# U units beside the context's score steps, and their Gelu in the expert stage

## The chip, the cores and the metric

The kernel runs on one core of one Trainium2 chip. The metric is the device time of one execution in microseconds (us), the median of some runs. The core has five engines, each with its own queue of instructions, worked off in order: TensorE (PE; its weight loads are shown apart as PEld), VectorE (DVE), ScalarE (ACT), GpSimd (POOL) and SyncE (SP), which issues most of the loads.

## The reference

Two blocks stand one after the other. The first has retention, a gated unit, and a layer of 16,384 experts of which every token uses 128. The second has two mixer layers, each with window attention, latent attention and a gated convolution, over 512 tokens and a context of 256. Its context doesn't depend on the first block.

```python
def block(hb):                       # the expert layer, over 128 tokens
    ...                              # expert, g: 8 heads x 16 experts, softmax
    ue = expert_u[expert]
    act = jax.nn.gelu(jnp.einsum('td,thkd->thk', hb, ue), approximate=False) * g
    ve = expert_v[expert]
    return jnp.einsum('thk,thkd->td', act, ve)

if update_ctx:                       # the first mixer layer's own work on the context
    ya_c = ctx_gqa_attn(qa_c.reshape(B, L, H_A, HD_A), kac, vac, sink)
    yb_c = ctx_mla_attn(qn_c, qr_c, kn_c, krb_c, vb_c)
    yc_c = short_gated_conv(bc_c, cc_c, uc_c, conv_w)
    out_c = merge_branches(ya_c, yb_c, yc_c, za_c, zb_c, zc_c, ga_c, gb_c, gc_c, w_branch, w_o)
```

## The kernel before

Every fp32 operand is split into a high and a low part, and every product is three matmuls (`mm3`, `fm`, L95). ScalarE casts the high part, and GpSimd or VectorE subtracts it to get the low one (`split`, L120 and L122).

The experts are computed densely for 384 of the tokens (TD) and sparsely, by gathered rows, for the other 128. The dense part has three stages. First `up_products` makes 128 *units* (U): for each block of 128 experts it loads 512 KB of weights in two parts (`wr<-eu`), splits them (`wh`, `wl`), makes 24 matmuls of 384 columns into `u`, and ScalarE evacuates them with a Gelu into `hb` (L745); two units' `hb` go to DRAM (`hd`). It is a generator, and each `next` issues one unit. Then `route` picks the experts and writes the gates to DRAM (`gd`). Last, `experts` runs 32 groups of four blocks: it loads gates `gt`, `ht` (four units' values from `hd`) and four tiles `vr`, multiplies `at = ht * gt`, splits `at` and `vr`, and adds up into eight PSUM banks `acc`.

Units are issued in the shadow of other work: `tick(n)` adds n to a counter and issues a unit for each whole one. `route` has its own amounts (R1 to R3). `context`, the first mixer layer's work on the context, runs between `route` and the experts: projections, convolution, gates, latent attention, gates, window attention, gates, output. Each weight product there asks for a PSUM bank by `mm()`, which ticks R4 = 0.53 and issues 0.95 sparse steps (`self.sparse`: a gather `sg` by GpSimd, and a multiply by VectorE, into `dots` or `sacc`). What units are left run after the context (`unit`, and the loop behind `cs.close()`). The two attentions are functions that the second block's layers call too; both take a `tick` of the caller's, and `context` gives none, so there the default does nothing.

A *score step* is one block of 128 queries of one head: score matmuls into `cs`, then on VectorE maximum `mx` and bias `nb`, on ScalarE the exponential `p` (L1124), on TensorE its transposition `ct` (L1138), which ScalarE and VectorE split into `pt`, and after two steps the weighting of the values `cv`. The context has 16 steps in each attention. ScalarE holds one set of functions at a time; an `ACT_TABLE_LOAD` stands where the next function is in another one than the last, as with Gelu and Exp.

A scheduling layer sets the final order on each engine: instructions that stand later in the code may go ahead of those that wait. Context weights are loaded into two buffers (`wrc`), split into `whc` and `wlc`, the latter by VectorE.

Of the kernel before, what the change touches and what calls it, by code (L numbers as in the profile page):

```python
# [14 lines left out]
AF = mybir.ActivationFunctionType  # L15
# [1 line left out]
AX = mybir.AxisListType  # L17
PSUM = bass.MemoryType.PSUM

R1, R2, R3, R4, R5, R6 = 0.5, 0.7, 0.6, 0.53, 0.9, 0.12  # L20
PC = 2
MB, MD, MR = 4, 2, 1.15
TG, NT = 4, 8
T = 512
TC = 256
# [3 lines left out]
TD = 384  # L29
# [38 lines left out]
class Kern:  # L68
# [507 lines left out]
    def experts(self):  # L576
        nc, a, h = self.nc, self.a, self.h
        self.fine = ("",)
        with ExitStack() as s1:
# [4 lines left out]
            ws = (up, 2 * PC, 3, "")  # L584
# [39 lines left out]
            ps = ExitStack()  # L624
            acc = [self.pool("pacc%d" % c, 1, PSUM, ps).tile([128, T], F32, name="acc%d" % c) for c in range(8)]

            for g in range(32):
                gt, ht = first if g == 0 else inputs(g)
                if g == 8:
                    self.load(x, self.x1d)  # L630
                ops = []
                for q in range(4):
                    raw = vp.tile([128, D], F32, name="vr", tag="vr", bufs=3)
                    self.load(raw, a["ev"][g * 4 + q])
                    vl = vp.tile([128, D], F32R, name="vl", tag="vl", bufs=4)
                    vh = vp.tile([128, D], F32R, name="vh", tag="vh", bufs=4)
                    self.split(vh, vl, raw, pool=False)
                    al = vp.tile([128, TD], F32R, name="al", tag="al", bufs=4)
                    at = vp.tile([128, TD], F32, name="at", tag="at", bufs=2)
                    nc.vector.tensor_tensor(at.rearrange("p (b t) -> p b t", t=32), ht[:, q, :].rearrange("p (b t) -> p b t", t=32),  # L640
                                            gt[:, :, q, :], op=OP.mult)
                    ah = vp.tile([128, TD], F32R, name="ah", tag="ah", bufs=4)
                    self.split(ah, al, at, pool=False)
                    ops.append((vh, vl, ah, al))
                    if g < 31:
                        for c in range(8):
                            cs = slice(c * 128, (c + 1) * 128)
                            self.mm3(acc[c][:, :TD], vh[:, cs], vl[:, cs], ah, al, g == 0 and q == 0, False)
                    self.sparse(S5)
# [82 lines left out]
    def up_products(self, ws, up, pu):  # L732

        for g in range(16):
            for q in range(4):
                hb = up.tile([128, 2, TD], F32, name="hb", tag="hb", bufs=2)
                for i in range(2):
                    w = self.wget(ws, self.a["eu"][g * 8 + q * 2 + i].rearrange("p (k n) -> p k n", k=8), 8, 128)
                    ps = pu.tile([128, T], F32, name="u", tag="u")
                    if self.last_units:  # L740
                        with self.tc.issue_after(self.pe_last()):
                            self.fm(ps[:, :TD], w, 0, 128, self.h, 0, TD)
                    else:
                        self.fm(ps[:, :TD], w, 0, 128, self.h, 0, TD)
                    self.nc.scalar.activation(out=hb[:, i, :], in_=ps[:, :TD], func=AF.Gelu)  # L745
                    if i == 1:
                        self.store(self.hd[g][:, 2 * q:2 * q + 2, :], hb)
                    yield
# [425 lines left out]
    def latent_attention(self, ws, l, sp, mm, sc, tp, pv, h, tq, kv, nk, kr, yy, bufs, pm, tick=lambda n: None):  # L1174

        nc = self.nc
# [7 lines left out]
        for j in range(2):  # L1184
            w = self.win(ws, l, "vb%d" % j)
            for n in range(0, nb, 2):
                ps = pm()
# [57 lines left out]
            nc.gpsimd.tensor_tensor(rot[0], rot[0], t, op=OP.add)  # L1245

        lag = 1 if tq == T else 0
        late = Later()

        def head(pr, e, n0, q, sz, rs):  # L1250
# [12 lines left out]

            for n in (n0, n0 + 1):
                qs = slice(n * 128, (n + 1) * 128)
                tick(R6)
                ps = sc()
                for lo, hi in spans:
                    self.mm3(ps[:, lo:hi], q[0][:, qs], q[1][:, qs], kt[0][:, lo:hi], kt[1][:, lo:hi], True, True)
                p = self.numer(sp, ps, 0, nk, SB, None, rs[:, n, e:e + 1])  # L1270
                late.now += 1
                late.after(lag, lambda n=n, p=p: turn(n, p))
                if n > n0:
                    late.after(2 * lag, values)
                late.run()
# [4 lines left out]
        for pr in range(4):  # L1280
            if pr == 1 and tq == T:
                self.dve_lo = ()
            if pr == 0:
                rope(0, pm)
                kn = keys(0, pm)
                ps = nope(0, pm)
# [62 lines left out]
    def window_attention(self, ws, l, sp, mm, sc, tp, pv, h, tq, kz, va, yy, bufs, tick=lambda n: None):  # L1349
        nc = self.nc  # L1350
# [18 lines left out]
            return self.silu2(ws, l, "za%d" % j, sp, "sza", bufs, mm, h, tq)  # L1369

        nq_, nsz = query(0), gate(0)
        tick(3)
        self.halves = False
        for j in range(4):
            q, sz = nq_, nsz
# [2 lines left out]
            for e in range(2):  # L1378
                sink = self.nsink[:, 8 * l + j + 4 * e:8 * l + j + 4 * e + 1]
                for n0 in range(0, nq, 2):  # L1380
# [3 lines left out]
                    for n in (n0, n0 + 1):  # L1384
# [11 lines left out]
                                mm_(ps[:, c:c + 128], self.identb, self.bmask[:, mi, :], start=False, stop=i == len(edge) - 1)  # L1396
                        for i in range(2):
                            mm_(ps[:, off:off + TC], q[e][:, qs], kz[e][i][:, off:off + TC], start=i == 0, stop=i == 1)
                        tick(R5)
                        slots = blocks + [vo, vo + 1]  # L1400
                        used.append(slots)
                        p = self.numer(sp, ps, lo, off + TC, SA, sink, rs[:, n, e:e + 1], es[:, n, e:e + 1])
# [43 lines left out]
    def context(self, ws, pu, tick, unit):  # L1446
        nc, a = self.nc, self.a
        with ExitStack() as s1:
# [20 lines left out]
            for l in range(1):  # L1469
# [9 lines left out]
                with ExitStack() as s2:  # L1479
# [27 lines left out]
                    self.conv(ws, l, sp, mm, h, TC, y)  # L1507
                    self.gates(ws, l, 2, True, mt, y, sp, mm, h, TC)
                    y = sp.tile([128, 2, 4, TC], F32R, name="cy", tag="cy")
                    self.latent_attention(ws, l, sp, mm, sc, tp, pv, h, TC, kv, TC, kr, y, 1, mm)  # L1510
                    self.gates(ws, l, 1, False, mt, y, sp, mm, h, TC)
                    kz = [[sp.tile([128, TC], F32R, name="ckz%d%d" % (i, k), tag="kt%d%d" % (i, k)) for k in range(2)] for i in range(2)]
                    self.pack_keys(kz, 0, TC, ka)
# [1 line left out]
                    for n in range(2):  # L1515
                        self.split(va[:, n, :, 0, :], va[:, n, :, 1, :], vf[:, n, :].rearrange("p (e c) -> p e c", e=2))
                    y = sp.tile([128, 2, 4, TC], F32R, name="cy", tag="cy")
                    self.window_attention(ws, l, sp, mm, sc, tp, pv, h, TC, kz, va, y, 1)
                    self.gates(ws, l, 0, False, mt, y, sp, mm, h, TC)
                    ot = sp.tile([128, 8, TC], F32, name="cot", tag="cy")  # L1520
                    x = sp.tile([128, 8, TC], F32, name="cx", tag="v", bufs=1)
# [416 lines left out]
```

## Time and profile before

| | us |
|---|---|
| median of 3 runs | 3709.58 (3703.13 to 3713.91) |
| the profiled execution | 3703.34 |
| its span | 3701.6 |
| route, to about | 1090 |
| context, about | 1090 to 1702 |
| last units, to | 1744 |
| experts, to about | 2290 |

The profile is of one execution. Its span goes from the first instruction to the last. TensorE's mean granted clock over it was 0.966 of full speed. Engines' busy times overlap, so that they don't add up to the span.

### The profile page before, as it was taken

How to read it: one execution, taken by the hardware profiler on the slowest of the kernel's cores; microseconds unless marked ns; L12 is line 12 of the kernel's file. 1: busy time of each engine (PE TensorE's matmuls, PEld its weight loads, DVE VectorE, ACT ScalarE, POOL GpSimd, SP SyncE). 2: the span in 40 equal slices, each digit the busy share in tenths (PEclk: the TensorE clock that was granted, in tenths of full speed). 3: DMA queues.
4: the chain of work that ended last, by engine and by line, in shares of the span. 5: the costliest groups of instructions: out<-in, count | busy, mean ns of one | idle time of the engine just before them, and what ended most of it. 6: DMA issues, size and time to landing. Idle time of an engine off the chain costs nothing.

```text
span 3701.6 us, 54609 instructions
## 1 busy us (share of the span) xinstructions
PE 3415.2 (92%) x20219; PEld 3074.3 (83%) x20219; DVE 2369.2 (64%) x4572; ACT 1564.2 (42%) x2940; POOL 1407.8 (38%) x1178
## 2 busy tenths in 40 slices
PE   6999999978889998897999999899999979999998
PEld 5889788877788988897999998778878877787777
DVE  7876865698867765666777775444255664433554
ACT  3323223235654374642333333444346443442663
POOL 2210114352235667565222211554425335542442
PEclk9999999989999998998999999999999989999999
DMA  7667644337877856578999993322211321212122
GB/s 274 217 204 263 219 159 152 107 125 269 298 265 242 301 194 241 184 273 294 355 342 337 327 328 111 103 69 69 77 52 55 134 82 63 75 67 67 54 72 99
DMA packets 273243, 668.18 MB, mean 181 GB/s; under 512 B 25424, under 2 KB 88016, under 8 KB 270160
## 3 DMA queue, kind: packets, MB, share of 16 engines
q1 hardware_dynamic: 220256, 469.43, 36.9%
q0 software_dynamic: 36864, 134.23, 10.1%
q10 hardware_dynamic: 15856, 61.02, 4.3%
q8 instruction: 159, 2.61, 0.3%
q14 instruction: 108, 0.88, 0.1%
HBM read 601.47 MB, written 63.11 MB: 180 GB/s over the span
## 4 chain that ended last, share of the span: by engine, by line
PE 65%; DVE 13%; DMA 7%; issue 7%; ACT 5%; POOL 3%; SPq 0%; POOLq 0%; ACTq 0%; DVEq 0%
PE mm L95 16%; PE acc L95 12%; PE gm L95 10%; PE u L95 8%; PE cm L95 4%; PE uq L95 2%; PE sc L95 2%; PE pv L1168 2%; DMA wr<-eu 2%; PE tp L1138 2%; PE pv L95 2%; PE tp L95 1%; DVE wm L212 1%; DVE wl L122 1%; POOL wl L122 1%
## 5 line engine op out<-in xcount | busy, mean ns | idle before, releaser
L122 POOL TENSOR_TENSOR wl<-wr,wh 128x512 fp32r<-128x512 f32 (+3 forms) x358 | 499.0, 1411 | 452.3 <-ACT wh L120 437.6
L120 ACT CAST wh<-wr 128x512 fp32r<-128x512 f32 (+3 forms) x546 | 355.8, 665 | 576.2 <-PE mm L95 201.5
L95 PE MATMUL u<-hh,wh 128*128 128x384 f32 (+1 forms) x1040 | 361.5, 348 | 31.8 <-ACT hb L745 31.6
L95 PE MATMUL u<-hh,wl 128*128 128x384 f32 (+1 forms) x1040 | 360.2, 347 | 9.7 <-DVE wl L122 8.9
L95 PE MATMUL u<-hl,wh 128*128 128x384 f32 (+1 forms) x1040 | 358.8, 345 | 0.0
L95 PE MATMUL acc<-ah,vh 128*128 128x384 f32 x1024 | 343.9, 336 | 8.8 <-ACT hb L745 8.8
L95 PE MATMUL acc<-al,vh 128*128 128x384 f32 x1024 | 343.3, 335 | 0.9 <-DVE al L122 0.9
L95 PE MATMUL acc<-ah,vl 128*128 128x384 f32 x1024 | 343.2, 335 | 0.0
L714 POOL DMA_INDIRECT sg<-ev,xid x128 | 153.3, 1198 | 311.4 <-DVE sacc L729 258.0
L120 ACT CAST vh<-vr 128x1024 fp32r<-128x1024 f32 x128 | 134.6, 1052 | 316.8 <-issue 145.0
L714 POOL DMA_INDIRECT sg<-ur,xid x128 | 146.8, 1147 | 270.2 <-DVE sg L212 250.7
L95 PE MATMUL mm<-hh,wh 128*128 128x512 f32 (+2 forms) x608 | 239.3, 398 | 9.1 <-DVE sm L432 4.2
L122 DVE TENSOR_TENSOR wl<-wr,wh 128x1024 fp32r<-128x1024 f32 (+4 forms) x188 | 179.5, 972 | 101.2 <-ACT wh L120 100.1
L95 PE MATMUL mm<-hh,wl 128*128 128x512 f32 (+2 forms) x608 | 238.9, 393 | 5.6 <-DVE wl L122 4.5
L95 PE MATMUL mm<-hl,wh 128*128 128x512 f32 (+2 forms) x608 | 238.8, 393 | 5.4 <-POOL hl L122 5.4
L122 DVE TENSOR_TENSOR vl<-vr,vh 128x1024 fp32r<-128x1024 f32 x128 | 158.3, 1237 | 128.4 <-ACT vh L120 126.9
L95 PEld LDWEIGHTS u<-hh,wh 128*128 128x128 f32 x1040 | 203.6, 196 | 34.8 <-ACT hb L745 32.9
L95 PEld LDWEIGHTS u<-hh,wl 128*128 128x128 f32 x1040 | 203.3, 196 | 13.1 <-DVE wl L122 11.3
L729 DVE SCALAR_TENSOR_TENSOR sacc<-sg,wts,sacc 128x1024 f32<-128x1024 f32 x128 | 189.3, 1479 | 22.5 <-DMA sg<-ev,xid 19.0
L95 PEld LDWEIGHTS u<-hl,wh 128*128 128x128 f32 x1040 | 203.4, 196 | 0.4
L95 PEld LDWEIGHTS acc<-ah,vh 128*128 128x128 f32 x1024 | 193.1, 189 | 9.3 <-ACT hb L745 9.1
L95 PEld LDWEIGHTS acc<-al,vh 128*128 128x128 f32 x1024 | 193.1, 189 | 1.1 <-DVE al L122 1.1
(713 smaller groups left out, 9837.2 us busy)
## 6 DMA issues: line engine op xcount, KB each, us to landing
wr<-eu SPq DMA_DIRECT2D x256, 256.0 KB
vr<-ev SPq DMA_DIRECT2D x128, 512.0 KB
wm<-wmod SPq DMA_DIRECT2D x88, 512.0 KB
wr<-w SPq DMA_DIRECT2D x164, 256.0 KB
wr<-wA SPq DMA_DIRECT2D x80, 512.0 KB
wrc<-w SPq DMA_DIRECT2D x79, 512.0 KB
wrg<-w SPq DMA_DIRECT2D x104, 256.0 KB
hd<-hb ACTq DMA_DIRECT2D x64, 384.0 KB
```

Of the source, the lines that this page charges most:

```text
L95: ins = self.nc.tensor.matmul(ps, l, r, start=first and i == 0, stop=last and i == 2)
L120: nc.scalar.copy(hi, x)
L122: eng.tensor_tensor(lo, x, hi.bitcast(F32), op=OP.subtract)
L212: return self.nc.vector.scalar_tensor_tensor(chunk, chunk, 1.0, row, op0=OP.mult, op1=OP.mult, accum_out=dst)
L714: self.here(nc.gpsimd.indirect_dma_start(t, None, tabs[i], bass.IndirectOffsetOnAxis(idx[:, j:j + 1], 0)))
L729: self.here(nc.vector.scalar_tensor_tensor(acc, t, wts[:, j:j + 1], acc, op0=OP.mult, op1=OP.add))
L1138: nc.tensor.transpose(t[:, (b - i) * 128:(b - i + 1) * 128], p[:, b * 128:(b + 1) * 128], self.ident)
L1168: nc.tensor.matmul(o[:, lo:hi], v(b), pt[k][:, b, lo:hi], start=i == 0 and k == 0, stop=i == len(parts) - 1 and k == 1)
```

## The change

The counter's amounts change, and score steps get one of their own, R9 = 1.0: `context` now hands its `tick` to both attentions. In the latent attention it issues a unit after the scores of each step, in the window attention too, and one ahead of the window attention. Each product of the context ticks 0.25 in place of 0.53. The evacuation of a unit becomes a copy, and the expert stage applies the Gelu to four blocks at once, in place, on the loaded `ht`. The other callers of the attentions keep what they had.

```diff
-R1, R2, R3, R4, R5, R6 = 0.5, 0.7, 0.6, 0.53, 0.9, 0.12
+R1, R2, R3, R4, R5, R6, R9 = 0.5, 0.7, 0.6, 0.25, 0.9, 0.12, 1.0
...
                 gt, ht = first if g == 0 else inputs(g)
+                nc.scalar.activation(out=ht, in_=ht, func=AF.Gelu)
...
-                    self.nc.scalar.activation(out=hb[:, i, :], in_=ps[:, :TD], func=AF.Gelu)
+                    self.nc.scalar.copy(hb[:, i, :], ps[:, :TD])
...
         lag = 1 if tq == T else 0
+        more = tick if tq < T else lambda n: None
         late = Later()
...
             for n in (n0, n0 + 1):
                 qs = slice(n * 128, (n + 1) * 128)
-                tick(R6)
+                if tq == T:
+                    tick(R6)
                 ps = sc()
                 for lo, hi in spans:
                     self.mm3(ps[:, lo:hi], q[0][:, qs], q[1][:, qs], kt[0][:, lo:hi], kt[1][:, lo:hi], True, True)
+                more(R9)
...
-        tick(3)
+        tick(3 if loc else 1)
...
-                        tick(R5)
+                        tick(R5 if loc else R9)
...
-                    self.latent_attention(ws, l, sp, mm, sc, tp, pv, h, TC, kv, TC, kr, y, 1, mm)
+                    self.latent_attention(ws, l, sp, mm, sc, tp, pv, h, TC, kv, TC, kr, y, 1, mm, tick)
...
-                    self.window_attention(ws, l, sp, mm, sc, tp, pv, h, TC, kz, va, y, 1)
+                    self.window_attention(ws, l, sp, mm, sc, tp, pv, h, TC, kz, va, y, 1, tick)
```

What this does to the order is best seen at three places. On TensorE, in the window attention (`cs` scores, `u` a unit, `ct` transpositions of `p`), two heads' scores stood together before, with 21 of a unit's matmuls behind them:

```order
L1398 MATMUL cs<-ckz_14404,aql 128x256
L1398 MATMUL cs<-ckz_14405,aql 128x256
L1398 MATMUL cs<-ckz_14404,aql 128x256
L1398 MATMUL cs<-ckz_14405,aql 128x256
L95 MATMUL u<-hh,wh 128x384
...
L95 MATMUL u<-hh,wl 128x384
L1138 MATMUL ct<-c_ident,p 128x128 x2
L1398 MATMUL cs<-ckz_14402,aqh 128x256
L1398 MATMUL cs<-ckz_14403,aqh 128x256
```

After the change each step's scores are followed by the 24 matmuls of one unit and then by that step's transpositions:

```order
L1402 MATMUL cs<-ckz_14219,aql 128x256
L1402 MATMUL cs<-ckz_14220,aql 128x256
L95 MATMUL u<-hh,wh 128x384
...
L95 MATMUL u<-hh,wl 128x384
L1139 MATMUL ct<-c_ident,p 128x128 x2
L1402 MATMUL cs<-ckz_14219,aql 128x256
L1402 MATMUL cs<-ckz_14220,aql 128x256
```

The units moved to between the scores and the transpositions that wait for them. On SyncE, in the projections and the convolution ahead of the first score step, the loads of context weights (`wrc`) and of units (`wr<-eu`) stood so before:

```order
L87 DMA wrc<-w 128x1024 x3
L87 DMA wr<-eu 128x512 x2
L87 DMA wrc<-w 128x1024 x8
L87 DMA wr<-eu 128x512 x2
L87 DMA wrc<-w 128x1024 x3
L87 DMA wr<-eu 128x512 x2
L87 DMA wrc<-w 128x1024 x2
L87 DMA wr<-eu 128x512 x2
```

And so after it:

```order
L87 DMA wrc<-w 128x1024 x3
L87 DMA wr<-eu 128x512 x2
L87 DMA wrc<-w 128x1024 x13
L87 DMA wr<-eu 128x512
L87 DMA wrc<-w 128x1024 x3
L87 DMA wr<-eu 128x512
L87 DMA wrc<-w 128x1024 x10
L87 DMA wr<-eu 128x512 x2
```

Unit loads went from one pair to two or three products to one pair to some thirteen. On ScalarE, where the units end and the experts begin (`ah`, `vh` are the experts' casts), the last three evacuations stood among the experts' casts before:

```order
L120 CAST wh<-wr 128x512
L120 CAST ah<-at 128x384 x2
L120 CAST vh<-vr 128x1024
L745 ACTIVATE hb<-u 128x384
L90 DMA hd_96<-hb 128x768
L120 CAST vh<-vr 128x1024 x2
L745 ACTIVATE hb<-u 128x384
L120 CAST ah<-at 128x384
L120 CAST vh<-vr 128x1024
L120 CAST ah<-at 128x384
L745 ACTIVATE hb<-u 128x384
```

After it they stand ahead of all of them, and the Gelu of `ht` is the first instruction of the experts:

```order
L746 COPY hb<-u 128x384 x2
L90 DMA hd_96<-hb 128x768
L629 ACTIVATE ht<-ht 128x1536
L120 CAST vh<-vr 128x1024
L120 CAST ah<-at 128x384 x2
L120 CAST vh<-vr 128x1024 x3
L120 CAST ah<-at 128x384 x2
L629 ACTIVATE ht<-ht 128x1536
```

The evacuations moved ahead of every expert cast, and the Gelus stand once a group.

## Rows read from the trace of the kernel before

**Rows 1.** The page: busy us (share of the span) and instructions by engine.

```profile
PE 3415.2 (92%) x20219; PEld 3074.3 (83%) x20219; DVE 2369.2 (64%) x4572; ACT 1564.2 (42%) x2940; POOL 1407.8 (38%) x1178
```

**Rows 2.** Windows: length, busy us by engine, granted clock, DMA share, GB/s.

```profile
1109.00:1323.00 214.00, 200.19 (x1430) 197.15 (x1429) 160.03 (x197) 91.28 (x167) 133.97 (x108) 0.97 0.77 264
1323.00:1414.00 91.00, 75.65 (x490) 69.93 (x488) 57.42 (x117) 66.33 (x141) 50.05 (x48) 0.91 0.57 195
1414.00:1488.00 74.00, 68.46 (x463) 67.43 (x463) 46.07 (x43) 26.05 (x44) 60.63 (x45) 0.92 0.73 262
1488.00:1563.00 75.00, 63.56 (x422) 58.86 (x422) 51.33 (x110) 54.43 (x123) 35.77 (x36) 0.93 0.51 171
1563.00:1666.00 103.00, 98.24 (x701) 97.23 (x699) 64.21 (x72) 47.04 (x84) 71.90 (x54) 0.98 0.75 260
1666.00:1744.00 78.00, 55.13 (x284) 52.39 (x284) 50.93 (x81) 22.71 (x45) 48.46 (x38) 0.86 0.77 283
1744.00:2290.00 546.00, 544.83 (x3157) 544.14 (x3157) 405.00 (x547) 192.99 (x273) 104.61 (x100) 0.99 0.87 309
```

**Rows 3.** TensorE's waits, 1109 to 1744: us in total, times, longest of one.

```profile
PE u L95 <- ACT hb L745: 9.1, 3, 8.2
```

**Rows 4.** TensorE's timeline: starts of a unit, a product, the next unit.

```profile
1178.29 0.34 PE L95 MATMUL u<-hh,wh 128*128 128x384 f32 x1
...
1182.45 0.28 PE L95 MATMUL cm<-ch,whc 128*128 128x256 f32 x1
...
1187.90 0.34 PE L95 MATMUL u<-hh,wh 128*128 128x384 f32 x1
```

**Rows 5.** SyncE's timeline, 1117 to 1163: loads issued, from and for how long.

```profile
1117.73 6.87 SPq L87 DMA_DIRECT2D wrc<-w  x3
1126.64 2.62 SPq L87 DMA_DIRECT2D wr<-eu  x2
1129.36 32.97 SPq L87 DMA_DIRECT2D wrc<-w  x8
```

**Rows 6.** TensorE's timeline: scores and their transpositions, two steps.

```profile
1506.00 0.63 PE L1398 MATMUL cs<-ckz,aql 128*128 128x256 f32 x4
...
1510.11 0.38 PE L1138 MATMUL ct<-c_ident,p 128*128 128x128 f32 x2
...
1533.57 0.40 PE L1398 MATMUL cs<-ckz,aql 128*128 128x256 f32 x2
...
1549.32 0.41 PE L1138 MATMUL ct<-c_ident,p 128*128 128x128 f32 x2 [0.35 <-DVE nb L1122]
```

**Rows 7.** Groups of ScalarE: count, busy us, mean ns, idle before.

```profile
L120 ACT CAST vh<-vr 128x1024 fp32r<-128x1024 f32 x128 | 134.6, 1052 | 316.8 <-issue 145.0 <-PE acc L95 121.1 <-DMA vr<-ev 50.8
...
L745 ACT ACTIVATE hb<-u 128x384 f32<-128x384 f32 x128 | 62.4, 487 | 49.9 <-PE u L95 49.0 <-ACT stg L906 0.8
...
L1124 ACT ACT_TABLE_LOAD x12 | 15.4, 1283 | 0.8 <-DVE nb L1122 0.6
```

**Rows 8.** ScalarE's timeline: a table load and what follows it.

```profile
1342.53 1.28 ACT L1124 ACT_TABLE_LOAD   x1
1343.82 0.47 ACT L1124 ACTIVATE p<-cs,nb 128x256 f32<-128x256 f32 x1
```

**Rows 9.** Timelines of TensorE, ScalarE and SyncE where the units end.

```profile
1713.89 1.11 SPq L87 DMA_DIRECT2D ht<-hd  x1
...
1724.97 0.98 ACT L120 CAST ah<-at 128x384 fp32r<-128x384 f32 x2 [8.36 <-issue]
...
1728.38 0.69 PE L95 MATMUL u<-hh,wh 128*128 128x384 f32 x1 [8.16 <-ACT hb L745]
...
1744.29 0.69 PE L95 MATMUL acc<-ah,vh 128*128 128x384 f32 x1 [8.78 <-ACT hb L745]
```

**Rows 10.** VectorE's groups, 1488 to 1563: a sparse step's multiply.

```profile
L212 DVE SCALAR_TENSOR_TENSOR sg<-sg,htok 128x1024 f32<-128x1024 f32 x5 | 8.3, 1669 | 0.0
```

**Rows 11.** VectorE's groups, 1780 to 2200: the same.

```profile
L212 DVE SCALAR_TENSOR_TENSOR sg<-sg,htok 128x1024 f32<-128x1024 f32 x39 | 47.4, 1216 | 0.0
```

## Prediction

> **What bounds the kernel now.** I read the page first: TensorE is busy for 92% of the span, the next engine for 64% [rows 1]. So the question is how much of TensorE's idle and slow time the change removes, and where it makes new idle time. TensorE's order of instructions is the same before and after the change up to the route's end (about 950 us) and again from the first expert matmuls on; only the context and the way into the experts differ. I therefore cut 1109 to 1744 us into six stretches in the table of windows [rows 2]: projections, convolution and gates (214 us), latent attention (91), gates (74), window attention (75), gates and output (103), the last units (78). The reader is to see that TensorE is busy for 200.2, 75.7, 68.5, 63.6, 98.2 and 55.1 us of them: 73.6 of 635 us are idle, over a third of that (15.3 + 11.4) in the two attentions and 22.9 at the end, and there the granted clock is below 1 too (0.91, 0.93, 0.86). In TensorE's list of waits the longest is that of U's matmuls for the evacuation hb, 9.1 us [rows 3].
>
> **Units of cost.** One unit (24 matmuls of 384 columns) takes TensorE from 1178.29 to 1182.45, 4.17 us; two weight products of the context (48 matmuls) take from there to 1187.90, 2.72 us each [rows 4]. But context weights don't come at that pace. Where the context ran almost without units, SyncE issued three product loads, two for one unit, then eight product loads from 1117.73 to 1162.33 [rows 5]: ten intervals in 44.3 us, less 2.7 us of unit loads, is 4.2 us a product. Loads have two buffers, and each waits for VectorE's split of the one before. This pace includes one stop; the eight loads alone are seven intervals in some 32.6 us, 4.66 us a product. The lower bound is TensorE's 2.72 us.
>
> **The change, stretch by stretch.** Counted in the two orders, units per stretch go from 20.3, 7.1, 7.9, 5, 11, 11 to 7.7, 18.6, 5, 18, 5, 8; the products stay, but for one that moves from the first stretch to the second.
>
> First stretch, 12.6 units fewer. TensorE needs 200.2 - 12.6 x 4.17 - 2.7 = 145 us, but now the loads bound it. Its first 31 us stand in the same order; then 28 products with only some four units among them take 28 x 4.2 = 118 us, in whose gaps (28 x 1.5 us) those units fit; the last bit before the first score falls from 29 to about 24 us. That is 173 us: -41. Bounds: -66 (TensorE alone) and -28 (4.66 us a product).
>
> Latent attention, 11.5 units and a product more: 75.7 + 11.5 x 4.17 + 2.7 = 126 us: +35. Window attention, 13 more: 63.6 + 13 x 4.17 = 118 us: +43. Here the idle time is what the units are to fill, so I add only work. The 75.7 and 63.6 us were partly run at a lower clock; full clock would give some 10 us back in each, and I let these stand for waits that are left. They will be left: a step now runs scores, 24 U matmuls, transposition in a fixed order, so 4.2 us of cover for the chain maximum, bias, exponential. Before, that chain took 3.5 us when quick (1506.63 to 1510.11) and 15.4 us when slow (1533.97 to 1549.32, with TensorE itself full in between) [rows 6]. The program's 29 table loads, 1283 ns each [rows 7], become 11 in the order; 22 lay in these 32 steps and four will, which frees 0.7 us of ScalarE a step. They are none of TensorE's own work, so they are no term of the sum, only a reason why the chain should fit.
>
> A load is followed at once by the next instruction (1342.53 + 1.28, next at 1343.82) [rows 8]. The Trainium skill (ScalarE: Activation LUTs, What ACT_TABLE_LOAD costs) puts a switch at 2.66 us, since it adds a drain of about 1.38 us to the 1283 ns. By that, an estimate, a step would be freed of 1.5 us, the 20 us of waits that I leave in the attentions would go, and the sum would be 20 us lower; the trace agrees on 1283 ns and shows no drain, so I go by the row.
>
> Gates after the latent attention, 2.9 units fewer: 68.5 - 12.1 = 56 us of TensorE, 12 products at 4.2 us are 50: 60 us with some of the old waits, -14. Gates and output, 6 fewer: TensorE 73 us, 18 products 76 us, and the waits at the output norm: 80 us, -23.
>
> The last units: three fewer at 4.17 us, -13. Then there is the entry into the experts. Before, ScalarE's first casts of the expert stage stood ahead of the last evacuations, and the cast ah waited 8.36 us for the ht load, issued at 1713.89; TensorE then stood 8.16 and 8.78 us behind hb [rows 9]. Now all hb copies stand ahead of the first expert work. What stays is the load itself, some 10 us from issue to use, of which the last unit hides half, and the fourth vr load: about 8 of 17 us, so -9. The first groups then run with less of a lead in loads: +4.
>
> The moved Gelu: 32 instructions of 128x1536 in place of none, and 128 evacuations that are copies. The trace shows no such form; its price lies between three halves of a 1.05 us cast of 128x1024 and four evacuations of 0.49 us [rows 7], 1.6 to 2.0 us, so 51 to 62 us on ScalarE, which is busy for 193 of the experts' 546 us [rows 2]. TensorE never waits there, and casts run up to four tiles ahead; I cost it at nothing. If that cover were gone it would be 1.6 us a group, 51 us. A copy instead of a Gelu costs the same to within the 0.49 us. The route's units change only in this.
>
> Sum: -41 + 35 - 14 + 43 - 23 - 22 + 4 = -18 us. The profiled execution took 3703.3 us, 6.2 us less than the median of 3709.6; taken off the median that gives 3691 us.
>
> **Rivals.** *Loss only moves.* The weight loads of the gates and the convolution, now with one unit to three or four products, run at 4.66 us a product and not at 4.2: 28 x 0.46 + 30 x 0.4 = 25 us more, +7 in all, 3716 us. For it: VectorE is busy for 160 of the first stretch's 214 us and the DMA engines for 77% [rows 2]. Against it: fewer unit loads and POOL splits compete there.
>
> *Slower: the step doesn't fit under one unit.* If maximum, bias and exponential take 4.2 + 1.7 us on average, 32 steps wait 54 us, 34 more than the 20 in the sum: +16, 3726 us. It decides from 1.2 us a step on. For it: VectorE's other work stands between maximum and bias, and it is slow where POOL splits weights: sg took 1669 ns in the window attention and 1216 ns among the experts [rows 10, 11]. The change puts 24.5 units' POOL splits beside the attentions. Against it: the loads are gone, and most slow chains of before had TensorE full ahead of the transposition. The Trainium skill (SBUF — State Buffer, Who interferes with whom) speaks for this rival: a VectorE instruction with two SBUF inputs and a POOL instruction that reads SBUF exclude each other. The trace agrees with these 1669 against 1216 ns.
>
> *A larger gain.* Products come at 3.6 us (halfway to TensorE's pace) and the attentions run at full clock without waits: -17 - 20 more, -55, 3655 us.
>
> **Numbers.** Forecast 0.45, loss only moves 0.25, slower 0.18, larger gain 0.12. What a measurement can tell from no change here is about 0.3%, 11 us. Faster than that: 0.85 of the forecast, all of the larger gain, little of the second: 0.52. Same: 0.15 of the forecast, three quarters of the second, a tenth of the third: 0.27. Slower: 0.21. The range goes from the larger gain to just past the slower rival, 3655 to 3730; the forecast's own is 3676 to 3706.
>
> **What would show it.** In the profile after: 11 table loads and not 29; first score at about 1282 us; the latent attention some 126 us long, the window attention 118; the expert matmuls without a stop from about 1722 us; TensorE's clock near 1 in both attentions and lower than 0.97 in the first stretch; SyncE waiting for VectorE's split wlc there. The prediction is wrong if the first stretch stays above 186 us, or if transpositions wait for p or nb by more than 1.2 us a step, or if the expert stage gets longer than 546 us.

## Result: the changed kernel is slower by 1.2%

| | before | after |
|---|---|---|
| median of 5 runs, us | 3705.02 (3699.36 to 3713.91) | 3747.57 (3735.15 to 3757.66) |
| the profiled execution, us | 3703.34 | 3757.66 |
| its span, us | 3701.6 | 3755.9 |

The ratio is 1.0119 (95% interval 1.01 to 1.0138). I forecast 3691 us, with a range of 3655 to 3730. The profiled execution of after is the slowest of its five, so the two traces lie 54.3 us apart where the medians lie 42.5 us apart.

The page of after: busy time by engine, and the lines of the chain of work that ended last, as shares of the span.

```profile
PE 3441.3 (92%) x20219; PEld 3089.8 (82%) x20219; DVE 2337.1 (62%) x4572; ACT 1580.6 (42%) x2954; POOL 1412.8 (38%) x1178
...
PE gm L95 10%; PE mm L95 8%; DMA ht<-hd 5%; PE u L95 4%; PE acc L95 4%; PE cm L95 2%; PE sc L95 2%; PE pv L1169 2%; PE tp L1139 2%; PE pv L95 2%; DVE vl L122 1%; PE tp L95 1%; DMA vr<-ev 1%; DMA wr<-w 1%; ACT vh L120 1%
```

Engine totals hardly differ from [rows 1]. But a load, `ht`, stands third on the chain with 5% of the span, which is far more than a kernel bound by TensorE should spend there.

The windows of after, cut as near as can be at the events that cut [rows 2] (columns as there; the busy times are those of PE, PEld, DVE, ACT and POOL):

```profile
1111.00:1299.00 188.00, 157.51 (x1106) 150.09 (x1106) 136.65 (x194) 71.86 (x127) 98.44 (x84) 0.93 0.73 252
1299.00:1423.00 124.00, 112.68 (x689) 108.61 (x689) 63.62 (x116) 65.36 (x158) 74.15 (x66) 0.94 0.57 180
1423.00:1495.00 72.00, 67.14 (x493) 65.55 (x492) 53.77 (x53) 29.27 (x48) 57.34 (x41) 1.00 0.84 285
1495.00:1597.00 102.00, 101.39 (x661) 98.78 (x661) 45.59 (x99) 55.93 (x141) 61.54 (x58) 1.00 0.60 195
1597.00:1692.00 95.00, 88.17 (x633) 86.14 (x631) 65.53 (x76) 40.89 (x74) 62.03 (x47) 0.95 0.79 273
1692.00:1751.00 59.00, 37.31 (x208) 36.48 (x208) 35.08 (x64) 16.36 (x32) 30.76 (x26) 0.85 0.68 240
1751.00:2350.00 599.00, 564.29 (x3159) 554.89 (x3159) 411.82 (x564) 239.12 (x310) 122.19 (x106) 0.97 0.80 290
```

The context (the first six) takes 640 us against 635. TensorE is idle in it for 75.8 us (640 less the six busy times) against 73.6 before. The window attention has almost no idle time left (102.00 long, 101.39 busy); the first stretch has more (30.5 us against 13.8). The expert stage (the last row) takes 599 us against 546, at a granted clock of 0.97 and a lower DMA share (0.80 against 0.87). Nearly all of the loss is there.

Waits in the expert stage of after, first TensorE's, then ScalarE's longest (us in total, times, longest):

```profile
PE acc L95 <- ACT ah L120: 40.8, 8, 17.5
PE acc L95 <- DVE al L122: 11.0, 16, 1.2
...
ACT ht L629 <- DMA ht<-hd: 240.6, 30, 13.7
```

The 17.5 us is the entry into the experts, just ahead of the window. The other stops are 40.8 - 17.5 + 11.0 = 34.3 us; the rest of the 53 us is longer busy time (564.3 us against 544.8 for as many matmuls), part of it at the lower clock. The last row points to the cause, which the experiments below test: ScalarE stood 240.6 us for its Gelus' loads.

In the context, the wait for `hb` of [rows 3] is down from 9.1 us to 1.4, and TensorE's longest in total is now that for VectorE's split of a product's weights (5.5 us before):

```profile
PE cm L95 <- DVE wlc L122: 15.7, 11, 4.7
```

The entry, to be set beside [rows 9]: timelines of ScalarE and TensorE. All units' copies are done, and the first Gelu, casts and matmul follow the landing of the first loads.

```profile
1747.46 1.48 ACT L629 ACTIVATE ht<-ht 128x1536 f32<-128x1536 f32 x1 [13.12 <-DMA ht<-hd]
...
1751.31 1.65 PE L95 MATMUL acc<-ah,vh 128*128 128x384 f32 x4 [17.50 <-ACT ah L120]
```

ScalarE's, TensorE's and SyncE's timelines of one group (start, length, in brackets the idle time before and what ended it):

```profile
1939.13 0.52 ACT L120 CAST ah<-at 128x384 fp32r<-128x384 f32 x1 [0.72 <-DVE at L641]
1952.31 1.48 ACT L629 ACTIVATE ht<-ht 128x1536 f32<-128x1536 f32 x1 [12.67 <-DMA ht<-hd]
1953.70 1.03 ACT L120 CAST vh<-vr 128x1024 fp32r<-128x1024 f32 x1
1954.63 0.51 ACT L120 CAST ah<-at 128x384 fp32r<-128x384 f32 x1
...
1955.19 0.69 PE L95 MATMUL acc<-ah,vh 128*128 128x384 f32 x1 [4.49 <-ACT ah L120]
...
1940.56 0.54 SPq L87 DMA_DIRECT2D ht<-hd  x1
1943.45 16.16 SPq L87 DMA_DIRECT2D vr<-ev  x3
1962.92 0.55 SPq L87 DMA_DIRECT2D ht<-hd  x1
```

Count the casts `vh`, four a group, from the stage's start: the Gelu at 1952.31 is that of group 12 (groups count from 0), but the cast behind it is the first of group 11. The Gelu stands a whole group ahead of its use. Its load was issued at 1940.56 and landed 11.7 us later; until then no cast could pass it in ScalarE's queue, and TensorE ran out of tiles at 1950.7. Over the 32 groups the Gelu stands ahead of three or four tiles of the group before 27 times, and directly ahead of its own only in the first three groups.

The chain of waits of after, 1930 to 1970, shows how this feeds itself:

```profile
1940.18 0.33 SPq L87
...
1940.56 11.72 DMA ht<-hd
1952.29 0.02 issue
1952.31 0.04 ACT ht L629
...
1953.70 1.04 ACT vh L120
1954.73 0.02 issue
1954.76 1.22 DVE vl L122
```

A `vl` split frees a `vr` buffer, so the next `vr` load is issued, behind it on SyncE the next `ht`; that lands some 10 us later and only then lets the next casts and splits run. So the Gelu's wait puts off the split that the next load waits for. A group takes 18.6 us instead of 16.6 (from the first `at` of group 12 to that of group 20, by eight).

### The profile page after: what moved, and what is told of

It is laid out like the page before. It is cut to its first block, busy times and chain, and to the rows that moved or that the text cites. A ratio compares the mean times of both kernels' runs of the same rounds, so it can differ in the third digit from the quotient of the medians.

```text
span 3755.9 us, 54574 instructions
## 1 busy us (share of the span) xinstructions
PE 3441.3 (92%) x20219; PEld 3089.8 (82%) x20219; DVE 2337.1 (62%) x4572; ACT 1580.6 (42%) x2954; POOL 1412.8 (38%) x1178
## 4 chain that ended last, share of the span: by engine, by line
PE 39%; DMA 9%; DVE 5%; issue 5%; ACT 3%; POOL 2%; SPq 0%; ACTq 0%; POOLq 0%; DVEq 0%
PE gm L95 10%; PE mm L95 8%; DMA ht<-hd 5%; PE u L95 4%; PE acc L95 4%; PE cm L95 2%; PE sc L95 2%; PE pv L1169 2%; PE tp L1139 2%; PE pv L95 2%; DVE vl L122 1%; PE tp L95 1%; DMA vr<-ev 1%; DMA wr<-w 1%; ACT vh L120 1%
## 5 line engine op out<-in xcount | busy, mean ns | idle before, releaser
L122 POOL TENSOR_TENSOR wl<-wr,wh 128x512 fp32r<-128x512 f32 (+3 forms) x358 | 490.9, 1386 | 436.6 <-ACT wh L120 420.0
L95 PE MATMUL acc<-ah,vh 128*128 128x384 f32 x1024 | 349.5, 342 | 40.8 <-ACT ah L120 40.8
L715 POOL DMA_INDIRECT sg<-ev,xid x128 | 164.6, 1286 | 368.0 <-DVE sacc L730 315.7
L95 PEld LDWEIGHTS acc<-al,vh 128*128 128x128 f32 x1024 | 196.7, 192 | 17.9 <-DVE al L122 17.7
L120 ACT CAST whc<-wrc 128x1024 fp32r<-128x1024 f32 (+3 forms) x108 | 106.3, 984 | 226.5 <-DMA wrc<-w 86.3
L95 PEld LDWEIGHTS acc<-ah,vl 128*128 128x128 f32 x1024 | 196.7, 192 | 0.0
```

The lines of the kernel that those rows point to most:

```text
L95: ins = self.nc.tensor.matmul(ps, l, r, start=first and i == 0, stop=last and i == 2)
L120: nc.scalar.copy(hi, x)
L122: eng.tensor_tensor(lo, x, hi.bitcast(F32), op=OP.subtract)
L715: self.here(nc.gpsimd.indirect_dma_start(t, None, tabs[i], bass.IndirectOffsetOnAxis(idx[:, j:j + 1], 0)))
```

## The experiments

Each ran in at least 3 rounds beside the kernel before; ratios are to it. "First stretch" is from the context's first product to its first score.

**Only the schedule.** The Gelu goes back to the units' evacuations.

```diff
-                nc.scalar.activation(out=ht, in_=ht, func=AF.Gelu)
...
-                    self.nc.scalar.copy(hb[:, i, :], ps[:, :TD])
+                    self.nc.scalar.activation(out=hb[:, i, :], in_=ps[:, :TD], func=AF.Gelu)
```

> Only the units' schedule is changed; the Gelu stays at the units' evacuations. Queue theory (the loss is the moved Gelu, which stands in ScalarE's queue ahead of casts of an earlier group and holds them until its own ht load lands): the 53 us by which the expert stage grew are gone, so some 3747 - 53 = 3694 us, with the context's 7 us of loss still there in part. Schedule theory (the units' new places leave the expert stage worse off, by its loads or its clock): the stage stays near 605 us and the time near 3745 us.

Measured: 3722.51 us, 1.0048 (1.0031 to 1.0065). The expert stage's growth is gone, as the queue theory had it, but the time is 28 us over the 3694 expected. ScalarE's table loads in the two attentions (1288 to 1602), with the instruction that each goes ahead of:

```profile
L745 ACT ACT_TABLE_LOAD x31 | 39.8, 1283 | 0.5
L1124 ACT ACT_TABLE_LOAD x26 | 33.4, 1283 | 2.8 <-DVE nb L1122 2.2
L1126 ACT ACT_TABLE_LOAD x5 | 6.4, 1283 | 0.1
```

With a Gelu between any two exponentials there are 62 of them, 79.5 us; before the change there were 22.

**Only the Gelu.** The units stand as before; the Gelu moves.

```diff
+                nc.scalar.activation(out=ht, in_=ht, func=AF.Gelu)
...
-                    self.nc.scalar.activation(out=hb[:, i, :], in_=ps[:, :TD], func=AF.Gelu)
+                    self.nc.scalar.copy(hb[:, i, :], ps[:, :TD])
```

> Only the Gelu is moved; the units stand in the context as before the change. Queue theory: the expert stage is some 50 us longer than the 552 us of before, and the time is about 3705 + 50 = 3755 us, less what the missing table loads in the attentions give back (0 to 22 us). Schedule theory: 3705 us or less.

Measured: 3746.05 us, 1.0109 (1.0091 to 1.0126). The moved Gelu alone gives the whole loss. The schedule theory falls.

**The Gelu pinned.** `here` keeps an instruction behind everything that was written before it for its engine.

```diff
-                nc.scalar.activation(out=ht, in_=ht, func=AF.Gelu)
+                self.here(nc.scalar.activation(out=ht, in_=ht, func=AF.Gelu))
```

> The changed kernel with one thing more: each Gelu of the expert stage is kept behind the last cast of the group before on ScalarE. The same 32 Gelus run on the same tiles. Queue theory: TensorE's stops for the cast ah (40.8 us) and for al (11 us) go to under 8 us together, the stage is 552 to 560 us and the time 3695 to 3703 us. Work theory (what costs is the Gelu's own 1.48 us a group, 47 us, because the casts have no slack for it): the stage stays above 595 us, the time above 3738 us.

Measured: 3704.26 us, 0.9993 (0.9983 to 1.0004). The same stage in this kernel, first its window:

```profile
1744.00:2290.00 546.00, 543.26 (x3136) 541.51 (x3137) 417.36 (x564) 240.22 (x309) 119.87 (x106) 1.00 0.89 318
```

It is as long as before, at full clock. The Gelus in ScalarE's groups (count, busy us, mean ns, idle before), of the changed kernel and then of the pinned one:

```profile
L629 ACT ACTIVATE ht<-ht 128x1536 f32<-128x1536 f32 x31 | 46.1, 1488 | 240.6 <-DMA ht<-hd 240.6
```

```profile
L629 ACT ACTIVATE ht<-ht 128x1536 f32<-128x1536 f32 x31 | 46.1, 1487 | 2.1 <-DMA ht<-hd 2.1
```

And a Gelu in the pinned kernel's timeline of ScalarE, behind the last cast of one group and ahead of the first of its own:

```profile
1949.78 0.51 ACT L120 CAST ah<-at 128x384 fp32r<-128x384 f32 x1
1950.19 1.49 ACT L629 ACTIVATE ht<-ht 128x1536 f32<-128x1536 f32 x1
1952.98 1.05 ACT L120 CAST vh<-vr 128x1024 fp32r<-128x1024 f32 x1 [1.31 <-issue]
```

The Gelus take the same 46.1 us of ScalarE, but wait 2.1 us and not 240.6. TensorE's stops from 1750 to 2290 (us in total, times, longest) are these alone:

```profile
PE acc L95 <- DVE al L122: 2.6, 3, 1.5
```

The median Gelu starts 19.4 us after its load was issued, against 10.3 in the changed kernel; a load of `ht` takes 9.9 us to land (median, in the run with the old schedule and pinned Gelus). The work theory falls: the Gelu's own time costs nothing that the ratio shows. Of the waits that I expected to go, the entry's own (17.5 us of the 40.8, now 14.6) stayed.

**No Gelu at all** (the changed kernel without its line in the expert stage, so that it leaves out the Gelu of the units altogether).

> The changed kernel with the Gelu of the U products left out altogether: neither at the evacuation nor in the expert stage. Its difference to the schedule alone is what the table loads in the context are worth. My prediction's step (0.7 us of ScalarE a step, no term of the sum): within 5 us of the schedule alone. Rival (the table loads hold the score chains): 10 to 22 us faster than the schedule alone.

Measured: 3704.05 us, 0.9993 (0.9984 to 1.0002): as with the pinned Gelu, and 18.5 us faster than the schedule alone. The rival holds: in the new schedule 62 table loads in the attentions, in place of 3, are worth some 18 us. With them ScalarE was busy for 93.8 of the window attention's 113 us, against 57.0 of 103 with the pinned Gelu (windows of the schedule alone, then of the pinned kernel):

```profile
1489.00:1602.00 113.00, 104.87 (x675) 101.44 (x674) 50.77 (x99) 93.77 (x169) 61.07 (x56) 0.98 0.48 160
```

```profile
1493.00:1596.00 103.00, 102.32 (x669) 99.52 (x667) 45.46 (x100) 56.95 (x143) 62.13 (x59) 1.00 0.58 193
```

This is no contradiction to my step, which set four table loads (three came) against the 22 of before; the next experiment tests that.

**The old schedule with the Gelu moved and pinned** (the only-Gelu kernel with `here`).

> The units stand where they stood before; the Gelu is moved to the expert stage and kept behind the last cast of the group before. It is the fourth corner of schedule by Gelu. If schedule and Gelu only add, the pinned Gelu with the new schedule (3704.3 us) less what the new schedule costs where no table loads stand in the attentions. My theory: the table loads of before (22 in the context) held the score chains, so 3695 us; rival: with the units of before in the context nothing waits for them, so 3705 us as before.

Measured: 3705.10 us, 0.9989 (0.9978 to 1.0). The rival holds: the 22 table loads of before cost nothing there that the ratio shows. Schedule by Gelu, in us:

| | at the evacuation | moved | moved and pinned |
|---|---|---|---|
| units as before | 3705 | 3746.05 | 3705.10 |
| units with the score steps | 3722.51 | 3747.57 | 3704.26 |

With the Gelu out of the way, the units' places make no difference that shows (ratios 0.9989 and 0.9993).

**More units for the entry.**

```diff
-R1, R2, R3, R4, R5, R6, R9 = 0.5, 0.7, 0.6, 0.25, 0.9, 0.12, 1.0
+R1, R2, R3, R4, R5, R6, R9 = 0.5, 0.7, 0.6, 0.25, 0.9, 0.12, 0.85
```

(on the pinned kernel)

> The pinned kernel with 0.85 unit a score step instead of 1: 13 units and not 8 stand behind the output norm. Theory of the entry: TensorE stands 14.6 us for the first cast ah because the first ht load can only be issued when the context's tiles are released, some 40 us after the norm; five units more (5 x 4.17 = 21 us) cover all of it, so the stretch stays at some 58 us with no stop and five units fewer stand in the attentions, where TensorE is full: -14 us, 3690 us. Rival: the attentions' own waits open up again or the loads of the further units put the ht load off, and the time stays at 3700 to 3706 us.

Measured: 3713.84 us, 1.0023 (1.001 to 1.0035). My theory falls, and the time is 8 us above even the rival's range. From its first score to its last product the context got shorter by 7.6 us, not by the 21 us of five units. And TensorE's stop moved from the first expert matmul into the units; TensorE's and ScalarE's timelines there:

```profile
1737.55 0.69 PE L95 MATMUL u<-hh,wh 128*128 128x384 f32 x1 [8.14 <-ACT hb L746]
...
1736.50 0.62 ACT L120 CAST wh<-wr 128x512 fp32r<-128x512 f32 x1 [8.30 <-DMA wr<-eu]
1737.02 0.47 ACT L746 COPY hb<-u 128x384 f32<-128x384 f32 x1
```

The units' weight loads now share the DMA engines with the experts' first loads, and a finished unit's copy stands in ScalarE's queue behind a cast that waits 8.30 us for such a load. It is the same kind of fault as the Gelu's: a wait for a load at the head of an in-order queue.

**Fine loads.** Weight products of the route and the context load in two halves (on the pinned kernel).

```diff
-        self.fine = ("",)
+        self.fine = ("", "c")
...
-            wc = (self.pool("wc", scope=cs), 2, 2, "c")
+            wc = (self.pool("wc", scope=cs), 2 * PC, 2, "c")
```

> The pinned kernel with each weight product of the route and the context loaded in two halves, in four buffers of half the size (the same memory). Theory of the product supply (two buffers, each held until VectorE's split, bound the stretches with few units): the first stretch falls from 179 us towards 165 us and the waits of cm for wlc (13.5 us) to under 5 us, the time by 10 to 25 us. Rival (DMA bandwidth itself or VectorE's work bound them): no change beyond 5 us.

Measured: 3688.22 us, 0.9947 (0.9935 to 0.996). The time fell as expected, but the first stretch only to 174.8 us, and TensorE's wait for `wlc` didn't fall (19.8 us in all against 13.5). So a control:

**The kernel before with fine loads.**

> The kernel before, with the weight products of the route and the context loaded in two halves as in the run with fine loads. Theory of the product supply: with some twenty units in the first stretch TensorE is full there (198.6 of 212.4 us) and supply hardly matters, so 3697 to 3705 us, at most 8 us faster than before, against the 16 us that the halves gave with the new schedule. Rival: halves help in the same way under either schedule (the route's end, the entry), 3689 us.

Measured: 3693.14 us, 0.9953 (0.9935 to 0.9971). The rival holds: halves help alike under both schedules. My theory that the loads' buffers held the new schedule back falls.

**Splits on POOL** (on the pinned kernel).

```diff
-            self.dve_lo = ("c",)
+            self.dve_lo = ()
```

> The pinned kernel with the context's splits wlc on POOL instead of VectorE. If VectorE's in-order queue paces the products (it is busy for 134 of the first stretch's 179 us, POOL for 93): the first stretch falls to 165 to 172 us and the time by 8 to 15 us. If the loads pace them (two buffers, ScalarE waits longest for the load): no gain in the first stretch, and POOL's slower split gives 0 to 20 us more.

Measured: 3785.51 us, 1.0209 (1.0188 to 1.0231). In the first stretch POOL's split of 128x1024 took 2442 ns against VectorE's 1253 in the pinned kernel, and TensorE waited 70.8 us for it in the context. POOL, busy for 178 of that stretch's 211 us, became the bound, and VectorE's own multiplies got slower too (`sg` 2574 ns against 1604), so that this says nothing on VectorE's queue.

**`ht` ahead of `gt`** (the two loads of `inputs` exchanged, on the kernel with fine loads).

> The kernel with fine loads, and in each group's loads the one of ht ahead of the one of gt. If the entry's stop (15 us for the first cast ah) is the landing of the first ht among the other loads of that moment: the stop falls by 2 to 3 us, the time to about 3686 us; if all of these loads together must land before the first group can run: no change from 3688 us.

Measured: 3689.58 us, 0.9942 (0.9925 to 0.996): no change. The first Gelu started 8 us sooner (1714.76 against 1722.69), and the cast `vh` behind it then waited 9.16 us for its `vr`. All first loads have to land.

**Earlier loads.** Three buffers for `ht` and `gt`, both asked for one group earlier (on the changed kernel, not pinned).

```diff
-                ht = vp.tile([128, 4, TD], F32, name="ht", tag="ht", bufs=2)
+                ht = vp.tile([128, 4, TD], F32, name="ht", tag="ht", bufs=3)
...
-                gt, ht = first if g == 0 else inputs(g)
+                gt, ht = first if g == 0 else nxt
+                nxt = inputs(g + 1) if g < 31 else None
```

> The changed kernel, Gelu not pinned, with three buffers instead of two for ht and gt and each group's two loads asked for one group earlier. The Gelu still stands in ScalarE's queue ahead of casts of the group before, but its load is meant to have landed by then. If it is the wait for the load that costs (queue theory): the expert stage comes down from 605 us to 552 to 565 us and the time to 3697 to 3712 us, though the Gelu stays ahead. If it is the place in the queue alone, or the Gelu's work: no change, 3740 to 3750 us.

Measured: 3746.26 us, 1.0112 (1.0094 to 1.0131). No gain, but not for the reason that I had set beside it: the wait I wanted to take away was still there, 230.6 us over the stage. The scheduling layer took the Gelu along with its load: it now stands seven or eight tiles ahead of its use, and still only 10.3 us behind its load's issue (median). Buffers don't help while the Gelu follows its load so closely; its place does.

**Middle rates** (0.38 unit a product, 0.6 a score step, on the kernel with fine loads).

> The kernel with fine loads and pinned Gelus with rates between the two schedules: 0.38 unit a product and 0.6 a score step (13 units in the first stretch, between 20 and 8). If idle time of TensorE in the context only moves from one place to another (some 70 us under either schedule): 3685 to 3692 us, as with the rates of the change. If each stretch is idle only where it has too few units, so that the middle serves both: 3670 to 3680 us.

Measured: 3677.38 us, 0.9928 (0.9912 to 0.9944). The interval just overlaps that of the fine loads alone, so that the gain is likely and not certain. The trace has the context (first product to first expert matmul) at 600.6 us against 613.4 with fine loads alone, and with a granted clock of 1.00 in four of its six stretches.

**Half the weight bytes** of the context (on the pinned kernel). Each product loads the first half of its weights and uses it twice; the kernel leaves out the other half.

```diff
+        half = tag == "c" and "c" in self.dve_lo and kc % 2 == 0
+        if half:
+            kc = c = kc // 2
...
-        return raw
+        return raw * 2 if half else raw
```

> The pinned kernel in which each weight product of the context loads only the first half of its weights and uses that half twice, in two casts and two splits (so the context computes with wrong weights; the instructions are those of the run with fine loads, and half the context's weight bytes are left out). The first stretch took 179 to 186 us in the runs with the new schedule and whole loads, 175 with halves. If the loads pace it (two buffers, bandwidth): it falls to 150 to 160 us, near TensorE's 153. If the chain of casts, VectorE's splits and the convolution's own work paces it: 170 to 175 us, as with halves.

**Fewer sparse steps** in the context (on the pinned kernel).

```diff
-S3, S4, SU, S5 = 0.8, 0.95, 1.2, 0.88
+S3, S4, SU, S5 = 0.8, 0.4, 1.2, 1.25
```

> The pinned kernel with 0.4 instead of 0.95 sparse step (a gathered row and VectorE's multiply of it) a product of the context, and 1.25 instead of 0.88 an expert tile, so that the same steps run later. VectorE is busy for some 134 of the first stretch's 179 us; some 15 to 20 steps of 1.2 to 1.7 us leave it, and as many gathers of 512 KB. If VectorE's queue paces the products: the first stretch falls to 160 to 170 us. If not: 176 to 185 us.

Measured: half the bytes 3686.82 us, 0.9962 (0.995 to 0.9973), first stretch 169.9 us; fewer sparse steps 3680.09 us, 0.9931 (0.9908 to 0.9955), first stretch 152.3 us. Windows in the first stretch, of half the bytes, then of fewer sparse steps:

```profile
1110.00:1280.00 170.00, 149.72 (x1091) 143.57 (x1091) 134.83 (x227) 72.00 (x159) 79.97 (x79) 0.96 0.63 212
```

```profile
1110.00:1262.00 152.00, 142.81 (x1085) 137.00 (x1083) 98.86 (x151) 67.67 (x119) 53.49 (x53) 0.99 0.64 216
1690.00:2246.00 556.00, 529.93 (x2988) 523.34 (x2988) 468.31 (x630) 233.17 (x296) 223.62 (x164) 0.98 1.00 369
```

Both leave the DMA engines the same room (0.63 and 0.64), but only the run that takes work off VectorE (98.9 us busy, against 133.4 in the pinned kernel's first stretch) brings TensorE close to full. So VectorE's queue paced the products, and not the loads. The same edit takes gathers off POOL (53.5 us busy against 92.9), and no run keeps the two apart; but TensorE's waits in the pinned kernel's first stretch are 10.5 us for VectorE's `wlc` and 1.0 us for POOL. The last row is the price: the expert stage then has a DMA share of 1.00 and takes 31.6 us more than with the pinned Gelu alone (first expert matmul to the transposition of the sparse sum, 555.8 against 524.2).

**A mild move of sparse steps** (`S4` 0.7, `S5` 1.05, with fine loads, pinned Gelus and middle rates).

> The pinned kernel with fine loads and the middle rates, with 0.7 sparse step a product and 1.05 an expert tile. With 0.4 and 1.25 the context was some 50 us shorter but the expert stage 31 us longer, its DMA engines busy all the time. If the first steps moved are the cheap ones (the expert stage had 11% of its DMA time left): 3655 to 3668 us, the expert stage 525 to 535 us. If each moved step costs there what it gives in the context: 3675 to 3682 us.

**Fewer sparse steps with the old places of the units** (pinned Gelus, whole loads).

> The units stand as before the change, Gelus pinned, with 0.4 sparse step a product and 1.25 an expert tile. If VectorE's queue is what kept the new places of the units from paying: under the old places TensorE itself fills the first stretch (198 us of work), which stays above 198 us, and the time is 3692 to 3705 us, some 12 to 25 us over the same with the new places (3680.1). If fewer sparse steps help alike under both: 3677 to 3685 us.

Measured: the mild move 3666.49 us, 0.9894 (0.9876 to 0.9912), below both kernels; the old places 3668.43 us, 0.99 (0.9883 to 0.9916), level with it. The second went against my expectation: the first stretch was 197.8 us and full, as I had said, but all stretches were shorter than in the old schedule with the pinned Gelu and all its sparse steps (the first had been 216.4 us; latent attention and gates 145.6 us against 157.0, the rest up to the output norm 165.2 against 182.1). Relief of VectorE pays under either schedule, and the new places of the units bring nothing even then: with them the same relief gave 3680.09 us (0.9931). So VectorE's queue explains the length of the first stretch, but not that the new places don't pay.

## Why the prediction was wrong

The traces, by the stretches of the prediction (an attention and the gates behind it taken together, since no single instruction parts them the same way in both kernels):

| stretch | predicted, us | measured, us |
|---|---|---|
| start of the context | 0 | +2.8 |
| projections, convolution, gates | -41 | -26.8 |
| latent attention, gates | +21 | +31.4 |
| window attention, gates, output | +20 | +18.8 |
| last units, entry | -22 | -19.2 |
| experts | +4 | +53.1 |
| rest | 0 | -5.8 |
| sum | -18 | +54.3 |

**The step that failed** is the one on the moved Gelu in the expert stage: "TensorE never waits there, and casts run up to four tiles ahead; I cost it at nothing." I costed what the Gelu does (1.6 to 2.0 us; it took 1.49) and not where it stands and what it waits for. An instruction that reads a fresh load holds all that is queued behind it. Before, the first reader of `ht` was VectorE's `at`, 17.7 us after the load's issue (median), and the casts `vh` needed no `ht`: that was the lead of four tiles. The Gelu put a reader of `ht` on ScalarE, ahead of those casts. I had shown its place in the first group alone, where it stands directly ahead of its own casts; from the sixth on it stands three or four tiles earlier. The stage took 599 us, past the 546 that I had named as a sign of being wrong; pinned, with the same Gelus, it took 546. That the loss is near the 51 us that I named for a lost cover is chance: that figure was the Gelu's own time, which the pinned kernel shows to cost nothing.

**Attentions.** That units cover the score chains was right: transpositions waited some 7 us for `sz` in 32 steps, far below 1.2 us a step, and the window attention ran without idle time, at a granted clock of 1.00, in 102 us and not 118; I had left 20 us of waits and the lower clock in the two. The latent attention and its gates took 10 us more than forecast: 16.2 of their 20.9 us of idle time stayed, where the sum left about 4, and the clock rose only from 0.91 to 0.94 in the attention itself. The 11 table loads came as counted, and as set against the 22 of before they were worth nothing that shows.

**The first stretch** was mis-sized: 26.8 us shorter, at the bound where products come at 4.66 us. The rival that the loss only moves was right on the outcome and wrong on the reason. It isn't the loads: half their bytes gave 169.9 us, where halves with all the bytes had given 174.8. It is VectorE's queue, 66 us of whose 133 there are the sparse steps' multiplies, with 16 us of idle time ahead of them for the gathers. In the pinned kernel and in the one with fewer sparse steps:

```profile
L212 DVE SCALAR_TENSOR_TENSOR sg<-sg,htok 128x1024 f32<-128x1024 f32 x22 | 35.3, 1604 | 3.0 <-DMA sg<-ur,xid 2.8 <-issue 0.2
L730 DVE SCALAR_TENSOR_TENSOR sacc<-sg,wts,sacc 128x1024 f32<-128x1024 f32 x21 | 30.9, 1470 | 13.0 <-DMA sg<-ev,xid 13.0
```

```profile
L212 DVE SCALAR_TENSOR_TENSOR sg<-sg,htok 128x1024 f32<-128x1024 f32 x9 | 11.0, 1219 | 0.0
```

**The entry** was right in sum (59 us against 56 forecast) and wrong in its course: the stop stayed whole (17.5 us) and three fewer units made up for it, and the experts' first matmul came at 1751.3 and not at 1722, since the stretches ahead were late.

So of the forecast's gain nothing shows in the medians: without the Gelu's wait, TensorE's idle time in the context is 69.0 us against 73.6 (lengths less busy times, pinned kernel), moved from the attentions into the first stretch. And the Gelu's wait cost 41 to 43 us on top by the medians, 53 us in the expert stage of the two traces. (Two slips in the working change nothing: the loads of [rows 5] went out in 44.6 us and not 44.3, which is still 4.2 us a product, and 3709.6 less 18 is 3692.)

What stays open: why the new places of the units bring nothing even with VectorE relieved; why halves of the loads give some 16 us under either schedule; and what a version would gain whose first expert loads are issued before the context's tiles are free, which no run tried.

## What to carry to other kernels

An operation moved to an idle engine costs nothing only if what it waits for is there when it comes up: look at its place in that engine's queue in a late group as well as in the first, at what stands behind it, and at how long before it its load is issued. If the order is made by a scheduler, pin the operation behind the work that doesn't need its load; more buffers alone let it run further ahead here. And before moving work into gaps of the busiest engine, ask who paces the stretch that it is taken from; here that was VectorE, and the gaps only moved.

## What the runs showed of the hardware

- In the expert stage a load of 768 KB took 9.9 us from issue to landing (median of 30), one of 512 KB 6.7 us (median of 121), in the run with the old schedule and pinned Gelus, at a DMA share of 0.92 (rows below: count, size, us from issue to landing). Gelus that started 10.3 us behind their load's issue (median, changed kernel) waited for it nearly each time, Gelus 19.4 us behind it (median, pinned) hardly ever.

```profile
vr<-ev SPq DMA_DIRECT2D x121, 512.0 KB, 6.7
...
ht<-hd SPq DMA_DIRECT2D x30, 768.0 KB, 9.9
```

- A stop of TensorE cost more than its own length: in the expert stage 34 us of stops went with 20 us more of busy time, at a granted clock of 0.97 instead of 0.99. After the stop of 4.49 us that ended at 1955.19, matmuls of 384 columns followed each other at 0.32 us until about 1961.5, and then at 0.17 as before the stop: the clock's lower level, then its higher one.
- VectorE's multiply `sg` took 1604 ns where POOL was busy for 93 of 179 us (pinned), 1219 ns where it was busy for 53 of 152 (fewer sparse steps), and 2574 ns where it was busy for 178 of 211 (splits on POOL). The Trainium skill (SBUF — State Buffer, Who interferes with whom) says that a VectorE instruction with two SBUF inputs and a POOL instruction that reads SBUF exclude each other; the trace agrees, as far as these three runs go.
